# Low parts moved to other engines and places in three stages, and half of the first mapped weights split, in a decoder block on one core

## The chip, the cores and the metric

The kernel runs on one core of a Trainium2 chip. The metric is the device time of one execution in microseconds (us), as the median of several runs. The engines are TensorE (PE, matmuls and transposes; PEld is its weight load), VectorE (DVE), ScalarE (ACT), GpSimd (POOL) and SyncE (SP, which issues most of the DMAs).

## The reference

One decoder block in f32 on a sequence of 1024 tokens of width 1024, with 16 heads of 64:

```python
mod = jax.nn.silu(c) @ w_ada + b_ada
shift, scale, gate = jnp.split(mod, 3, axis=-1)
h = rms_norm(x, norm_gain) * (1.0 + scale[:, None, :]) + shift[:, None, :]
q, k, v, z_a, u, z_b, m_a, m_b = jnp.split(h @ w_in, offs, axis=-1)
attn = stick_breaking_attention(to_heads(q), to_heads(k), to_heads(v))
p_a = (attn * jax.nn.silu(z_a)) @ w_branch_a
pooled = multiscale_causal_pool(u, pool_w, pool_scale)
p_b = (pooled * jax.nn.silu(z_b)) @ w_branch_b
merged = jax.nn.sigmoid(m_a) * p_a + jax.nn.sigmoid(m_b) * p_b
return x + gate[:, None, :] * (merged @ w_out)
```

Behind the block stands a last RMS norm with its own gain. The pooling takes trailing means over 2, 4, 8 and 16 tokens, minus the token itself, then one 256x256 map for each of four groups of channels (`pool_w`).

## The kernel before

**Precision.** Nearly every matmul is made of three products. An f32 operand is split into a high part (a cast to fp32r, most often on ACT) and a low part (the f32 value less the high part, a subtraction on DVE or POOL), and PE computes high x high, high x low and low x high into one PSUM bank. So a block of weights can be used in part as soon as it is cast, and in full when its low part is there. In the names, `w_3_raw` is a block as loaded, `w_3` holds its two parts, and a row such as `wa<-wa_raw,wa` on DVE makes the low part. All matmuls are issued in one helper, at L99, so rows are told apart by their tiles.

**The front.** Four blocks of x (`x_0` to `x_3`, 128 tokens each) are loaded, squared and summed on ACT (`junk<-x`), raised to -0.5 by POOL (L245, `st`), scaled on DVE (`x<-x,st`), turned by PE in sets of four transposes (`xt`), and made into `hf` and the high part of `hT` by ACT, with the low part of `hT` by DVE. `mods` are the columns of the modulation, which DVE sums up in two operations per block of channels (`mj`), and for which ACT computes a sigmoid (`sigb`). Meanwhile PE folds the maps of the pooling into the weights of `u`: for each group g of 256 channels, `mapped(g, q, tag)` for q = 0 to 3 makes 256 columns (`wm_q`), two halves of weights (`wt_0` for q = 0, 1 and `wt_1` for q = 2, 3) against the map `praw`. ACT and DVE split each result into `wg`. Groups 0 and 1 are computed in whole f32 (`WHOLE = 2`), groups 2 and 3 in three fp32r products. The first accumulation over the eight blocks of channels, `ua`, starts when the first `hT` and `wg` are there. The front is written out by hand: `order(...)` keeps the instructions of each engine in the order of the program as long as `pinned[0]` is set. PSUM has four tags of two banks: `pj`, `z`, `av`, `tr`; `ua0` to `ua3` take `pj`, `pj`, `z`, `z`.

**Middle stages.** The projections of u and v follow, then the pooled branch (`pb`), in which the low parts of later weights are made ahead by `make_lo` and put into memory (`wl_d`). Attention runs over eight pairs of heads; its logits `z` go through two sigmoids on ACT (`om`, `be`), a select on POOL (L802), a scan on DVE (L804, `om<-om`) and a multiplication on DVE. The projections of the pairs run beside it; `load_parts(i)` loads weight tile i, and tiles below `PLAIN` are split there, low part on POOL (L114, `w<-w_raw,w`).

**The last stage.** For each half of the tokens (`sh` 0 and 1) and each j from 0 to 7, `load_w` loads and splits `wa_j`, three loads bring `s_j`, `m_j` and `b_j`, PE computes `pa_j` from `ga` and `wa_j` (24 matmuls, of which the third is the first to need `wa_j`'s low part), and DVE forms `m_j`·`b_j` + `pa_j`·`s_j` and splits it into `mhl_j`. Then the output product `o` runs from `mhl` and `wo`, with a last norm for each block of 128 tokens: `y`, squares on ACT (`t`), sums (`qq`), a power on POOL (L1014) and two multiplications on DVE (L1019). In the first half `wo` is scaled by the gate (`wor`) and split as well. The order of these instructions on each engine isn't written by hand: a scheduler sets it from its own estimate of times, and so do the buffers of the pools: a tile with `bufs=2` can't be loaded until the last reader of the tile two before is done.

Of the kernel before, what the change touches and what calls it, by code (L numbers as in the profile page):

```python
# [9 lines left out]
F32 = mybir.dt.float32  # L10
# [5 lines left out]
P = 128  # L16
# [19 lines left out]

PLAIN = 8
LO_V = (1, 0, 1, 1, 0, 1, 1, 0)
LO_ZB = (0, 1, 0, 1, 0, 1, 0, 1)
# [6 lines left out]

WHOLE, G2 = 2, 1
BUSY = 10
# [7 lines left out]
def block_kernel(ctx, tc, a, out):  # L56
    nc = tc.nc
# [5 lines left out]
    const = ctx.enter_context(pool("const"))  # L63
    big = ctx.enter_context(pool("big"))
    wts = ctx.enter_context(pool("wts"))
    dram = ctx.enter_context(tc.tile_pool(name="dram", bufs=1, space=bass.MemoryType.DRAM))
# [13 lines left out]

    ident = const.tile([P, P], F32, name="ident")
    make_identity(nc, ident)
    ones = const.tile([P, P], F32, name="ones")
    gp.memset(ones, 1.0)
# [52 lines left out]

    def make_lo(pl, n, tag=None, bufs=3):

        for _ in range(n):  # L140
            i = next(early_lo)
            if tag:
                raw, hi = (pl.tile([P, D], t_, tag=tag, bufs=5, name=f"l{i}_{n_}") for n_, t_ in (("raw", F32), ("hi", F32R)))
            else:
                raw = pl.tile([P, D], F32, tag="lraw", bufs=bufs, name=f"l{i}_raw")
                hi = pl.tile([P, D], F32R, tag="lhi", bufs=1, name=f"l{i}_hi")
            nc.sync.dma_start(raw, a["w_in"][tiles[i]])
            act.copy(hi, raw)
            v.tensor_sub(raw.bitcast(F32R), raw, hi.bitcast(F32))
            nc.sync.dma_start(wl_d[i], raw)  # L150
# [51 lines left out]
    with pool("init") as init:  # L202

        affb = const.tile([P, 8], F32, name="affb")
        v.scalar_tensor_tensor(affb, bada_v[:, 8:16], 1.0, gain_v, ALU.add, ALU.mult)

        crow = init.tile([P, D], F32, tag="vjunk", bufs=1, name="crow")[0:1]
        nc.sync.dma_start(crow, a["c_row"])
# [32 lines left out]
        def square_x(sb):  # L241
# [37 lines left out]
        xts = {}  # L279

        def turn_x(sh, kb):
            pt = xts[sh, kb] = bank(("tr", "av")[kb % 2], f"xt{sh}_{kb}")
            for i in range(4):
                transpose(pt[:, i * P:(i + 1) * P], xs[4 * sh + i][:, kb * P:(kb + 1) * P])
# [18 lines left out]

        wg, maps, halves = {}, {}, {}

# [9 lines left out]

        def split_map(g):
            hl = init.tile([P, 2, 2, 256], F32R, tag="phl", bufs=1, name=f"phl{g}")
            order(act.copy)(hl[:, 0], maps[g])
            order(v.tensor_sub)(hl[:, 1], maps[g], hl[:, 0].bitcast(F32))
            maps[g] = hl  # L320

# [5 lines left out]

        def mapped(g, q, tag):
# [4 lines left out]
            th, ml = halves[g, q // 2], maps[g]  # L333
            for e in range(2):
                ks = slice((2 * q + e) % 4 * P, (2 * q + e) % 4 * P + P)

                pairs = [(th[:, cb, ks], ml[:, cb]) for cb in range(2)] if g < WHOLE else [
                    (th[:, i, cb, ks], ml[:, j, cb]) for i, j in ((0, 0), (0, 1), (1, 0)) for cb in range(2)]
                for n, (l, r) in enumerate(pairs):
                    mm(ps[:, e * 256:e * 256 + 256], l, r, start=n == 0, stop=n == len(pairs) - 1)  # L340

            def out(which=(0, 1)):
                dst = wg[g][:, :, 2 * q:2 * q + 2].rearrange("p i k d -> p i (k d)")
                if 0 in which:
                    order(act.copy)(dst[:, 0], ps)
                if 1 in which:
                    order(v.tensor_sub)(dst[:, 1], ps, dst[:, 0].bitcast(F32))
            return out

# [60 lines left out]
        load_mod(4)  # L410
        low_h(0, 0, v)
        m13(lo_)
        make_h(0, 1, None)
# [3 lines left out]
        sl = slice(0, 512)  # L417

        def cast(g, hf):
            raw = halves[g, hf]  # L420
            hl = halves[g, hf] = wts.tile([P, 2, 2, 512], F32R, tag="whl", bufs=2, name=f"wt{g}_{hf}")
            order(act.copy)(hl[:, 0], raw)
            return lambda: order(v.tensor_sub)(hl[:, 1], raw, hl[:, 0].bitcast(F32))

        def cast_map(g):
            raws[g] = maps[g]
            maps[g] = init.tile([P, 2, 2, 256], F32R, tag="phl", bufs=1, name=f"phl{g}")
            order(act.copy)(maps[g][:, 0], raws[g])

        def low_map(g):  # L430
            order(v.tensor_sub)(maps[g][:, 1], raws.pop(g), maps[g][:, 0].bitcast(F32))

        raws = {}

# [10 lines left out]
        for kb in range(KB):  # L445
# [56 lines left out]
            if kb == KB - 2:  # L502

                turned = [init.tile([P, 4, 512], F32, tag="wa", bufs=3, name=f"xt{i}") for i in range(2)]
                for i in range(2):
                    load(turned[i].rearrange("p k s -> p (k s)"), a["x_t"][i])
                split_map(3)
                for hf in range(2):
                    split_half(3, hf)
# [33 lines left out]

    def make_d(j):
        win = WINDOWS[j // 2]
        u = dif.tile([P, S + 16], F32, tag="u", bufs=2, name=f"u{j}")
        v.memset(u[:, S:], 0.0)
        nc.sync.dma_start(u[:, :S], u_d[j])
        cur, n, step = u, S + 16, 1
# [12 lines left out]


    with pool("vp") as vp:
# [11 lines left out]
        early.close()  # L576
        diffs = ExitStack()
        dif = diffs.enter_context(pool("dif", side="right"))
        for hf in range(2):
            if hf == 0:  # L580
                wv.append([load_wv(1, k2) for k2 in range(4)])
            for sb in range(8):
# [15 lines left out]
                )  # L598
                make_lo(vp, LO_V[sb])
                if 8 * hf + sb in DIFFS:  # L600
                    make_d(DIFFS[8 * hf + sb])


    with pool("pb") as pb:
        gb = pb.tile([P, 2, KB, S], F32R, name="gb")
        for j in range(KB):
            if j not in dhls:
                make_d(j)
            zs = [pb.tile([P, 512], F32, tag="zs", bufs=3, name=f"zs{j}_{sh}") for sh in range(2)]
# [333 lines left out]
    with pool("fin") as fin:  # L943
# [138 lines left out]
```

## Time and profile before

| | us |
|---|---|
| median of 3 runs | 1212.78 (1212.56 to 1213.09) |
| the profiled execution | 1212.4 |
| its span in the trace | 1210.4 |
| PE busy | 1199.6 (99%) |
| DVE busy | 757.9 (63%) |
| ACT busy | 540.6 (45%) |
| POOL busy | 193.8 (16%) |

The granted TensorE clock was 0.999 of full speed. A row of the time line gives start and duration in us, the engine, the line, the operation, what it writes and reads, the sizes and how many instructions are merged (x16); in brackets stands the time that the engine was idle just before, and what ended that. A list of waits gives for each pair of waiter and releaser the sum in us, the number of times and the longest.

### The profile page before, as it was taken

What the parts mean: (1) busy time and instruction counts of PE and PEld (TensorE: products, weight loads), DVE (VectorE), ACT (ScalarE), POOL (GpSimd) and SP (SyncE); (2) the same over time, 40 slices, a digit from 0 to 9 for tenths busy, and PEclk for the clock granted to TensorE, in tenths of its full rate; (3) what the DMA queues carried; (4) which work ended last, traced back from release to release, by engine and by line L of the source; (5) the groups of instructions that cost most, each with busy time, mean ns of one, the idle gap of its engine ahead of it and who ended that gap; (6) DMA issues with size and microseconds to landing.
All of it is one profiled execution on the core that took longest, in us unless ns stands there. A gap on an engine that the chain in (4) does not pass through costs nothing.

```text
span 1210.4 us, 16174 instructions
## 1 busy us (share of the span) xinstructions
PE 1199.6 (99%) x5746; PEld 1000.1 (83%) x5746; DVE 757.9 (63%) x1049; ACT 540.6 (45%) x1008; POOL 193.8 (16%) x361
## 2 busy tenths in 40 slices
PE   8999999999999999999999999999999999999997
PEld 7888888888888888888888888888888888888886
DVE  6764482677410277767768677776777763785643
ACT  5564341334211265665556655655655653232211
POOL 1000000001222343212212122231211310000001
PEclk9999999999999999999999999999999999999999
DMA  9649994626846632442635325353343236984622
GB/s 361 255 168 339 326 383 167 214 82 230 317 148 117 179 92 75 133 121 78 170 109 157 113 80 153 109 158 115 106 132 102 96 126 211 315 275 168 218 65 84
DMA packets 81955, 207.13 MB, mean 171 GB/s; under 512 B 10450, under 2 KB 23890, under 8 KB 79699
## 3 DMA queue, kind: packets, MB, share of 16 engines
q1 hardware_dynamic: 73666, 191.23, 49.2%
q10 hardware_dynamic: 8208, 14.88, 3.3%
q8 instruction: 45, 0.74, 0.2%
q14 instruction: 36, 0.29, 0.1%
HBM read 138.96 MB, written 50.34 MB: 156 GB/s over the span
## 4 chain that ended last, share of the span: by engine, by line
PE 93%; DVE 2%; DMA 2%; issue 1%; ACT 0%; POOL 0%; SPq 0%; POOLq 0%; DVEq 0%; ACTq 0%
PE p L99 36%; PE pb L99 7%; PE wzb L99 7%; PE v L99 7%; PE o L99 6%; PE av L99 6%; PE z L99 6%; PE wt L99 5%; PE pa L99 5%; PE u L99 5%; PE ua L99 3%; PE wm L99 1%; DMA m<-sb_d 1%; DMA out_y<-y 0%; DMA praw<-in_pool_w 0%
## 5 line engine op out<-in xcount | busy, mean ns | idle before, releaser
L99 PE MATMUL p<-hT,w 128*128 128x512 f32 x1920 | 480.9, 392 | 0.0
L99 PEld LDWEIGHTS p<-hT,w 128*128 128x128 f32 x1920 | 354.8, 188 | 68.6
L804 DVE TENSOR_TENSOR_SCAN om<-om 128x512 f32<-128x512 f32 (+7 forms) x128 | 175.4, 1370 | 50.0 <-ACT om L797 41.5
L824 DVE TENSOR_TENSOR wt<-wt,wt 128x512 fp32r<-128x512 f32 (+1 forms) x160 | 100.5, 628 | 93.7 <-ACT wt L823 93.1
L823 ACT CAST wt<-wt 128x512 fp32r<-128x512 f32 (+1 forms) x160 | 87.5, 547 | 130.2 <-PE wt L99 129.7
L797 ACT ACTIVATE om<-z 128x512 f32<-128x512 f32 (+2 forms) x192 | 94.9, 494 | 77.2 <-PE z L99 52.2
L802 POOL TENSOR_SCALAR_AFFINE_SELECT om<-om 128x128 f32<-128x128 f32 x128 | 50.9, 397 | 364.3 <-ACT om L797 344.0
L99 PE MATMUL av<-wt,vv 128*128 128x512 f32 x320 | 106.0, 412 | 0.0
L99 DVE TENSOR_TENSOR be<-be,om 128x511 f32<-128x511 f32 (+7 forms) x128 | 95.8, 758 | 0.3
L798 ACT ACTIVATE be<-z 128x512 f32<-128x512 f32 (+2 forms) x192 | 94.2, 491 | 0.0
L99 PE MATMUL pa<-ga,wa 128*128 128x512 f32 x384 | 89.9, 390 | 0.3 <-DVE s L976 0.2
L99 PEld LDWEIGHTS wt<-ident,be 128*128 128x128 f32 x576 | 72.7, 140 | 20.9
L99 PE MATMUL o<-wo,mhl 128*128 128x512 f32 (+1 forms) x408 | 89.6, 377 | 0.0
L99 PE MATMUL wt<-ident,be 128*128 128x128 f32 x576 | 88.7, 272 | 0.0
L99 PE MATMUL v<-wv,hT 128*128 128x512 f32 x384 | 87.2, 389 | 0.0
L99 PE MATMUL wzb<-hT,wzb 128*128 128x512 f32 x384 | 87.2, 389 | 0.0
L99 PE MATMUL pb<-gb,wb 128*128 128x512 f32 x384 | 87.2, 389 | 0.0
L99 PEld LDWEIGHTS o<-wo,mhl 128*128 128x128 f32 x408 | 73.5, 188 | 14.1
L99 PEld LDWEIGHTS pa<-ga,wa 128*128 128x128 f32 x384 | 71.9, 188 | 15.9 <-issue 0.6
L99 PEld LDWEIGHTS v<-wv,hT 128*128 128x128 f32 x384 | 72.1, 188 | 14.9
L99 PEld LDWEIGHTS wzb<-hT,wzb 128*128 128x128 f32 x384 | 72.1, 188 | 14.9
L99 PEld LDWEIGHTS pb<-gb,wb 128*128 128x128 f32 x384 | 72.1, 188 | 14.9
(129 smaller groups left out, 1374.2 us busy)
## 6 DMA issues: line engine op xcount, KB each, us to landing
w_raw<-in_w_in SPq DMA_DIRECT2D x40, 512.0 KB, 4.8
l_raw<-in_w_in SPq DMA_DIRECT2D x32, 512.0 KB, 5.1
wl_d<-l_raw SPq DMA_DIRECT2D x32, 512.0 KB, 5.8
w<-wl_d SPq DMA_DIRECT2D x32, 512.0 KB, 3.9
v_d<-vo SPq DMA_DIRECT2D x16, 512.0 KB, 4.8
vv<-v_d SPq DMA_DIRECT2D x8, 1024.0 KB, 5.5
wa_raw<-in_w_branch_a SPq DMA_DIRECT2D x16, 512.0 KB, 4.8
wa<-in_w_mod SPq DMA_DIRECT2D x7, 1024.0 KB, 6.5
```

The source lines that it names most:

```text
L99: ins = op(*args, **kw)
L797: act.activation(om[:, b0:b0 + n], zp[:, :n], AF.Sigmoid, scale=-0.125)
L798: act.activation(be[:, b0:b0 + n], zp[:, :n], AF.Sigmoid, scale=0.125)
L802: gp.affine_select(out=tl[:, :P], in_=tl[:, :P], pattern=[[1, P]], compare_op=ALU.is_gt, fill=fill, base=0, channel_multiplier=-1)
L804: v.tensor_tensor_scan(om[:, :W], om[:, :W], om[:, :W], 1.0, ALU.mult, ALU.min)
L823: act.copy(wt[:, 0, :off], pt[:, :off])
L824: v.tensor_sub(wt[:, 1, :off], pt[:, :off], wt[:, 0, :off].bitcast(F32))
```

## The change

Six edits, in four places.

**Front.** A sigmoid of a small constant tile stands ahead of everything on ACT, so that its table is loaded at the start. The map of group 0 and its second half of weights are split into fp32r parts (`WHOLE` is now a list of the halves that stay whole); the first scaling of x goes from DVE to ACT; the last two mapped blocks of group 1 take the banks `av` and `tr` of the first two transposes instead of two of `z`; the second half of the last block is computed behind the first transposes, and the split of `wm_2` is moved in part behind `hT`'s first low part.

**v stage.** `make_lo` can give back its cast and subtraction to be issued one block later, and the loads of `make_d` are issued one block sooner.

**Attention.** The low part of weight tile 4 is made by DVE instead of POOL.

**Last stage.** `s_`, `m_` and `b_` have three buffers each.

```diff
+MASKED = 4
-WHOLE, G2 = 2, 1
+WHOLE = ((0, 0), (1, 0), (1, 1))
...
     def load_parts(i, name):
         if i < PLAIN:
-            return load_w(a["w_in"][tiles[i]], name, act, gp)
+            return load_w(a["w_in"][tiles[i]], name, act, v if i == MASKED else gp)
...
+        act.activation(mhalf, mhalf, AF.Sigmoid)
+        gp.memset(mhalf, -0.5)
...
+        def scale_act(sb):
+            order(act.mul)(xs[sb], xs[sb], stats[sb][:, 2:3])
...
-        mapped(0, 0, "pj")()
+        m00 = mapped(0, 0, "pj")
+        cast_map(0)
+        low_map(0)
+        m00()
+        t0_lo = cast(0, 1)
         m01 = mapped(0, 1, "pj")
+        t0_lo()
         m01(hi)
         square_x(0)
         m01(lo_)
         spread()
-        scale_x(0)
+        scale_act(0)
...
-        m12 = mapped(1, 2, "z")
-        m13 = mapped(1, 3, "z")
+        for kb in range(2):
+            bank_x(0, kb)
+        m12 = mapped(1, 2, "av")
+        m13 = mapped(1, 3, "tr", (0,))
         square_x(3)
+        m12(hi)
         scale_x(3, some)
         turn_x(0, 0)
         scale_x(3, rest)
         turn_x(0, 1)
-        m12()
         make_h(0, 0, None)
+        m13.products((1,))
         m13(hi)
         modulation(1)
         load_mod(4)
         low_h(0, 0, v)
+        m12(lo_)
         m13(lo_)
...
-                make_lo(vp, LO_V[sb])
+
+                now, todo = todo, make_lo(vp, LO_V[sb], later=True)
                 if 8 * hf + sb in DIFFS:
-                    make_d(DIFFS[8 * hf + sb])
+                    j = DIFFS[8 * hf + sb]
+                    todo.append(lambda j=j, u=load_u(j): make_d(j, u))
+                for f in now:
+                    f()
...
-                s_ = fin.tile([P, 512], F32, tag="s_", bufs=2, name=f"s{sh}_{j}")
+                s_ = fin.tile([P, 512], F32, tag="s_", bufs=3, name=f"s{sh}_{j}")
...
-                m_ = fin.tile([P, 512], F32, tag="m_", bufs=2, name=f"m{sh}_{j}")
+                m_ = fin.tile([P, 512], F32, tag="m_", bufs=3, name=f"m{sh}_{j}")
...
-                b_ = fin.tile([P, 512], F32, tag="b_", bufs=2, name=f"b{sh}_{j}")
+                b_ = fin.tile([P, 512], F32, tag="b_", bufs=3, name=f"b{sh}_{j}")
```

The following rows show the order of instructions. On PE in front, at the end of group 1's mapped blocks, before:

```order
L99 MATMUL wm_2_227<-praw_128,wt_130 128x256 x4
L99 MATMUL wm_3_232<-praw_128,wt_130 128x256 x4
L99 MATMUL xt_0_242<-ident,x_113 128x128
...
L99 MATMUL xt_1_248<-ident,x_116 128x128
L99 MATMUL ua_273<-hT,wg_143 128x512 x2
L99 MATMUL ua_274<-hT,wg_143 128x512 x2
```

and after:

```order
L103 MATMUL wm_2_256<-praw_133,wt_135 128x256 x4
L103 MATMUL wm_3_261<-praw_133,wt_135 128x256 x2
L103 MATMUL xt_0_254<-ident,x_118 128x128
...
L103 MATMUL xt_1_255<-ident,x_121 128x128
L103 MATMUL wm_3_261<-praw_133,wt_135 128x256 x2
L103 MATMUL ua_300<-hT,wg_148 128x512 x2
L103 MATMUL ua_301<-hT,wg_148 128x512 x2
```

Half of `wm_3` stands behind the two sets of transposes now, ahead of the first `ua`.

On DVE in the first half of the last stage, around the low part of `wa_3`, before:

```order
L977 TENSOR_TENSOR m_1_9509<-m_1_9509,s_1_9507 128x512
L123 CAST mhl_1_9541<-m_1_9509 128x512
L114 TENSOR_TENSOR wa_3_9588<-wa_3_raw,wa_3_9588 128x1024
L114 TENSOR_TENSOR mhl_1_9541<-m_1_9509,mhl_1_9541 128x512
L948 TENSOR_TENSOR wor_9628<-wor_9628,bg 128x1024
L948 TENSOR_TENSOR wor_9675<-wor_9675,bg 128x1024
L950 TENSOR_TENSOR wo<-wor_9628,wo 128x1024
L114 TENSOR_TENSOR wa_4_9635<-wa_4_raw,wa_4_9635 128x1024
L950 TENSOR_TENSOR wo<-wor_9675,wo 128x1024
L976 TENSOR_TENSOR s_2_9549<-pa_2_9556,s_2_9549 128x512
```

and after:

```order
L1018 TENSOR_TENSOR m_1_9536<-m_1_9536,s_1_9534 128x512
L1010 TENSOR_TENSOR m_2_9578<-m_2_9578,b_2_9580 128x512
L127 CAST mhl_1_9568<-m_1_9536 128x512
L118 TENSOR_TENSOR mhl_1_9568<-m_1_9536,mhl_1_9568 128x512
L1017 TENSOR_TENSOR s_2_9576<-pa_2_9583,s_2_9576 128x512
L118 TENSOR_TENSOR wa_3_9615<-wa_3_raw,wa_3_9615 128x1024
L989 TENSOR_TENSOR wor_9655<-wor_9655,bg 128x1024
```

`s_2<-pa_2` stood seven operations behind the low part of `wa_3`; it stands directly ahead of it now.

On DVE at the start of the second half, around the low part of `wa_2`, before (`y` is the last of the first half's four output blocks):

```order
L1003 TENSOR_TENSOR y_10074<-o_1_10106,y_10074 128x512
L976 TENSOR_TENSOR s_0_10145<-pa_0_10152,s_0_10145 128x512
L977 TENSOR_TENSOR m_0_10147<-m_0_10147,s_0_10145 128x512
L114 TENSOR_TENSOR wa_2_10226<-wa_2_raw,wa_2_10226 128x1024
L1011 SCALAR_TENSOR_TENSOR qq_10076<-qq_10076 128x1
...
L1019 SCALAR_TENSOR_TENSOR y_10074<-y_10074,qq_10076,fg 128x512 x2
```

and after:

```order
L1044 TENSOR_TENSOR y_10101<-o_1_10133,y_10101 128x512
L1017 TENSOR_TENSOR s_0_10172<-pa_0_10179,s_0_10172 128x512
L1052 SCALAR_TENSOR_TENSOR qq_10103<-qq_10103 128x1
L1018 TENSOR_TENSOR m_0_10174<-m_0_10174,s_0_10172 128x512
L1060 SCALAR_TENSOR_TENSOR y_10101<-y_10101,qq_10103,fg 128x512 x2
L118 TENSOR_TENSOR wa_2_10253<-wa_2_raw,wa_2_10253 128x1024
```

`qq` and the two `y` multiplications, which wait for POOL's power, stood behind the low part of `wa_2`; they stand ahead of it now. The edit of the v stage moves no instruction on any engine.

## Rows read from the trace of the kernel before

**Rows 1.** The page, part 1: busy us, share of the span, instructions.
```profile
PE 1199.6 (99%) x5746; PEld 1000.1 (83%) x5746; DVE 757.9 (63%) x1049; ACT 540.6 (45%) x1008; POOL 193.8 (16%) x361
```

**Rows 2.** The list of waits of PE: us in total, times, longest.
```profile
PE ua L99 <- ACT hT L99: 1.1, 1, 1.1
PE ua L99 <- DVE wg L99: 1.0, 1, 1.0
PE z L99 <- ACT be L798: 0.4, 1, 0.4
PE pa L99 <- DVE s L976: 0.2, 1, 0.2
```

**Rows 3.** The time line of PE in front.
```profile
15.12 7.07 PE L99 MATMUL wm<-praw,wt 128*128 128x256 f32 x32
...
22.03 1.04 PE L99 MATMUL xt<-ident,x 128*128 128x128 f32 x8
24.15 1.66 PE L99 MATMUL ua<-hT,wg 128*128 128x512 f32 x6 [1.08 <-ACT hT L99]
...
30.93 3.01 PE L99 MATMUL ua<-hT,wg 128*128 128x512 f32 x12
...
39.74 1.59 PE L99 MATMUL wm<-phl,wt 128*128 128x256 f32 x12
```

**Rows 4.** Tile x from 0 to 24 us: its loads, issue ns and first and last issue.
```profile
L234 SPq DMA_DIRECT2D x<-in_x x4: 328/431/463, 3.0 to 8.7; - x4
...
DMA to landing us min/median/max: 5.7/8.5/10.0
```

**Rows 5.** The time line of DVE in front.
```profile
13.34 1.29 DVE L99 TENSOR_TENSOR scb<-crow,sigb 128x512 f32<-128x512 f32 x2 [2.26 <-ACT sigb L99]
14.54 0.74 DVE L99 TENSOR_SCALAR x<-x,st 128x1024 f32<-128x1024 f32 x1
...
19.68 1.21 DVE L99 SCALAR_TENSOR_TENSOR mj<-wa,scb 128x1024 f32<-128x1024 f32 x1
...
21.67 0.88 DVE L99 TENSOR_SCALAR x<-x,st 128x128 f32<-128x128 f32 x2
...
29.08 0.69 DVE L99 TENSOR_TENSOR hT<-hf,hT 128x512 fp32r<-128x512 f32 x1
```

**Rows 6.** The time line of ACT in front.
```profile
19.26 1.06 ACT L99 ACTIVATE junk<-x 128x1025 f32<-128x1025 f32 x1
...
22.67 0.78 ACT L99 ACTIVATE hf<-xt,mods 128x512 f32<-128x512 f32 x1 [1.58 <-PE xt L99]
...
30.43 0.62 ACT L99 CAST hT<-hf 128x512 fp32r<-128x512 f32 x1
```

**Rows 7.** The time line of POOL: the power in front and in the last stage.
```profile
20.49 0.81 POOL L245 TENSOR_TENSOR st<-st,mhalf 128x1 f32<-128x1 f32 x1 [2.56 <-ACT junk L99]
...
1127.46 0.66 POOL L1014 TENSOR_TENSOR qq<-qq,mhalf 128x1 f32<-128x1 f32 x1 [6.88 <-DVE qq L1011]
```

**Rows 8.** The time lines of POOL and DVE early in attention.
```profile
426.85 2.40 POOL L114 TENSOR_TENSOR w<-w_raw,w 128x1024 fp32r<-128x1024 f32 x1 [0.20 <-ACT w L119]
...
429.53 1.02 DVE L804 TENSOR_TENSOR_SCAN om<-om 128x384 f32<-128x384 f32 x1 [2.39 <-POOL om L802]
```

**Rows 9.** The time line of PE in the last stage, from 1039 us on.
```profile
1038.74 11.95 PE L99 MATMUL pa<-ga,wa 128*128 128x512 f32 x52
```

**Rows 10.** The time line of DVE in the last stage, first half.
```profile
1039.84 0.69 DVE L976 TENSOR_TENSOR s<-pa,s 128x512 f32<-128x512 f32 x1 [1.20 <-PE pa L99]
...
1043.05 1.22 DVE L114 TENSOR_TENSOR wa<-wa_raw,wa 128x1024 fp32r<-128x1024 f32 x1
```

**Rows 11.** The time line of DVE in the last stage, start of the second half.
```profile
1124.16 0.69 DVE L1003 TENSOR_TENSOR y<-o,y 128x512 f32<-128x512 f32 x1 [4.75 <-PE o L99]
...
1126.10 1.22 DVE L114 TENSOR_TENSOR wa<-wa_raw,wa 128x1024 fp32r<-128x1024 f32 x1
...
1129.97 1.41 DVE L1019 SCALAR_TENSOR_TENSOR y<-y,qq,fg 128x512 f32<-128x512 f32 x2
```

More of the change, by code (lines that the diff above doesn't have):

```diff
@@ L64, in block_kernel @@
     big = ctx.enter_context(pool("big"))
+    idp = ctx.enter_context(pool("idp"))
     wts = ctx.enter_context(pool("wts"))
@@ L79, in block_kernel @@
     wl_d = dram.tile([5 * KB, P, D], F32, name="wl_d")
-    ident = const.tile([P, P], F32, name="ident")
+    ident = idp.tile([P, P], F32, name="ident")
     make_identity(nc, ident)
-    ones = const.tile([P, P], F32, name="ones")
+    ones = idp.tile([P, P], F32, name="ones")
     gp.memset(ones, 1.0)
@@ L136, in block_kernel, with make_lo @@
     early_lo = iter(range(PLAIN, len(tiles)))
-    def make_lo(pl, n, tag=None, bufs=3):
+    def make_lo(pl, n, tag=None, bufs=3, later=False):
+        rest = []
         for _ in range(n):
@@ L147, in make_lo, with low @@
             nc.sync.dma_start(raw, a["w_in"][tiles[i]])
-            act.copy(hi, raw)
-            v.tensor_sub(raw.bitcast(F32R), raw, hi.bitcast(F32))
-            nc.sync.dma_start(wl_d[i], raw)
+            def low(i=i, raw=raw, hi=hi):
+                act.copy(hi, raw)
+                v.tensor_sub(raw.bitcast(F32R), raw, hi.bitcast(F32))
+                nc.sync.dma_start(wl_d[i], raw)
+            if later:
+                rest.append(low)
+            else:
+                low()
+        return rest
     def load_parts(i, name):
         if i < PLAIN:
-            return load_w(a["w_in"][tiles[i]], name, act, gp)
+            return load_w(a["w_in"][tiles[i]], name, act, v if i == MASKED else gp)
         raw = wts.tile([P, KB, P], F32, tag="raw", bufs=2, name=name + "_raw")
@@ L279, in block_kernel, with bank_x @@
         xts = {}
+        def bank_x(sh, kb):
+            xts[sh, kb] = bank(("tr", "av")[kb % 2], f"xt{sh}_{kb}")
         def turn_x(sh, kb):
-            pt = xts[sh, kb] = bank(("tr", "av")[kb % 2], f"xt{sh}_{kb}")
+            if (sh, kb) not in xts:
+                bank_x(sh, kb)
+            pt = xts[sh, kb]
             for i in range(4):
@@ L302, in block_kernel @@
         tags = ("pj", "pj", "z", "z", "av", "tr")
-        wg, maps, halves = {}, {}, {}
+        wg, maps, parts_m, halves = {}, {}, {}, {}
         def load_map(g):
@@ L314, in load_half, with cast_map, low_map, cast @@
             halves[g, hf] = raw.rearrange("p (c k) -> p c k", c=2)
[L316 to L320, printed above, removed]
+        def cast_map(g):
+            parts_m[g] = init.tile([P, 2, 2, 256], F32R, tag="phl", bufs=1, name=f"phl{g}")
+            order(act.copy)(parts_m[g][:, 0], maps[g])
+        def low_map(g):
+            order(v.tensor_sub)(parts_m[g][:, 1], maps[g], parts_m[g][:, 0].bitcast(F32))
+        def cast(g, hf):
+            raw = halves[g, hf]
+            hl = halves[g, hf] = wts.tile([P, 2, 2, 512], F32R, tag="whl", bufs=2, name=f"wt{g}_{hf}")
+            order(act.copy)(hl[:, 0], raw)
+            return lambda: order(v.tensor_sub)(hl[:, 1], raw, hl[:, 0].bitcast(F32))
         def split_half(g, hf):
@@ L326, in split_half, with mapped @@
             order(v.tensor_sub)(hl[:, 1], raw, hl[:, 0].bitcast(F32))
-        def mapped(g, q, tag):
+        def mapped(g, q, tag, es=(0, 1)):
             if g not in wg:
@@ L332, in mapped, with products @@
             ps = bank(tag, f"wm{g}_{q}")
[L333 to L340, printed above, removed]
+            th = halves[g, q // 2]
+            whole = (g, q // 2) in WHOLE
+            ml = maps[g] if whole else parts_m[g]
+            def products(es):
+                for e in es:
+                    ks = slice((2 * q + e) % 4 * P, (2 * q + e) % 4 * P + P)
+                    pairs = [(th[:, cb, ks], ml[:, cb]) for cb in range(2)] if whole else [
+                        (th[:, i, cb, ks], ml[:, j, cb]) for i, j in ((0, 0), (0, 1), (1, 0)) for cb in range(2)]
+                    for n, (l, r) in enumerate(pairs):
+                        mm(ps[:, e * 256:e * 256 + 256], l, r, start=n == 0, stop=n == len(pairs) - 1)
+            products(es)
             def out(which=(0, 1)):
@@ L347, in out @@
                     order(v.tensor_sub)(dst[:, 1], ps, dst[:, 0].bitcast(F32))
+            out.products = products
             return out
@@ L417, in block_kernel @@
         sl = slice(0, 512)
[L419 to L433, printed above, removed]
         def hi_products(todo):
@@ L506, in block_kernel @@
                     load(turned[i].rearrange("p k s -> p (k s)"), a["x_t"][i])
-                split_map(3)
+                cast_map(3)
+                low_map(3)
                 for hf in range(2):
@@ L542, in block_kernel, with load_u @@
     dhls = {}
-    def make_d(j):
-        win = WINDOWS[j // 2]
+    def load_u(j):
         u = dif.tile([P, S + 16], F32, tag="u", bufs=2, name=f"u{j}")
@@ L548, in make_d @@
         nc.sync.dma_start(u[:, :S], u_d[j])
+        return u
+    def make_d(j, u):
+        win = WINDOWS[j // 2]
         cur, n, step = u, S + 16, 1
@@ L577, in block_kernel @@
         diffs = ExitStack()
+        todo = []
         dif = diffs.enter_context(pool("dif", side="right"))
@@ L598, in block_kernel @@
                 )
-                make_lo(vp, LO_V[sb])
+                now, todo = todo, make_lo(vp, LO_V[sb], later=True)
                 if 8 * hf + sb in DIFFS:
-                    make_d(DIFFS[8 * hf + sb])
+                    j = DIFFS[8 * hf + sb]
+                    todo.append(lambda j=j, u=load_u(j): make_d(j, u))
+                for f in now:
+                    f()
+        assert not todo
     with pool("pb") as pb:
```

2 lines of the change are left out of this document (1 added, 1 removed).

## The prediction

> **What bounds the kernel now.** I read the page's busy shares first, then the list of who TensorE (PE) waits for, then the stretches of the time line around each of those waits. PE is busy 1199.6 us of the 1210.4 us span [rows 1]: a change can only bring what is left of PE's idle time, or shorten PE's own work. The list of its waits [rows 2] has few entries that an order of instructions can move: 1.1 us at the first products of `ua` (for `hT`, from ACT), 1.0 us a little later (for a `wg` part, from DVE), 0.4 us in attention (for `be`) and 0.2 us in the last stage (for `s`). Between them PE runs without a gap, so what is gained or lost at one place reaches the end in full, unless DVE or a load gives it back at once. The pace of PE in the last stage is (11.95 - 0.39)/51 = 0.227 us per 128x512 matmul [rows 9]; one takes 0.39 from start to end.
>
> **The front (0 to 45 us).** PE's own work: `wm_2` and `wm_3` of group 0 go from 16 f32 records to 24 in fp32r. 32 f32 records took 7.07 us and 12 fp32r ones 1.59 [rows 3], so 3.5 becomes 3.0, -0.5. The same row gives 0.22 per f32 record, and four of them (`wm_3`'s second half) leave the stretch ahead of the transposes, another -0.9 there; they are done while PE waits for `hT`, which is the cover. PE would thus reach the first transposes at about 20.6 instead of 22.03 [rows 3]. It can't use all of that. The fourth x block is issued at 8.7 and lands 10.0 later [rows 4], at 18.7; its Square and the read behind it end 1.25 later (1.06 and some 0.2, [rows 6]), its power takes POOL 0.81 [rows 7]; that is 20.8, and DVE is then just through `wg` and scales the first 128 columns by 21.2 (before: from 21.67, [rows 5]). The transpose ends at 21.5, the ACT step `hf` starts there instead of at 22.67 [rows 6], and the first `ua` product, which stood 1.48 behind it [rows 3, 6], comes at 23.0 instead of 24.15: -1.15. The next wait, 1.00 for DVE's `wg` [rows 2], was for the bank of the last map block; that block now has another bank, so this wait goes and a gain of 2.15 would stand at 27 us.
>
> What is late next is DVE's chain of `mj`, `hT` and `wg` operations, which has no gap from 21.67 on. DVE loses one scaling (0.74) to ACT; the two operations it gains (the low parts of the map and of the weights, by their sizes 0.69 and 1.22, [rows 10]) fall into its idle time ahead of `scb`, of which the last piece alone was 2.26 us [rows 5], so they cost nothing. One `wg` part, some 0.69 by its size, is moved behind the first `hT` low part. With the 0.5 by which the last scaling comes sooner, that first `hT` part comes 1.2 earlier, but from the next one on, with the `wg` part made up for, DVE is only some 0.55 ahead of before. The second `hT` low part, which ended at 29.77 [rows 5], then ends at 29.2, while PE is there at 23.0 + 24 products and two sets of transposes (5.4 + 0.7) at 28.5 to 29.1 with its own wait for the second high part: a stall of 0.3 to 0.7. The third high part, whose cast ended at 31.05 [rows 6], ends at 30.5, and PE wants it at 30.1. Its first products after that come at 30.5, where before they came four matmuls behind 30.93 [rows 3], at 31.84. I keep -1.3 for the front. The bounds are -0.55 (PE tied to DVE all the way) and -2.15. The second table load of ACT and the moved scaling are off the path: ACT waits 1.58 for PE ahead of `hf` [rows 6].
>
> **The v stage.** The helper that holds back the low parts by one block gives the same sequence on every engine between the front and attention. Zero.
>
> **Attention.** `w_4`'s low part moves from POOL, where it took 2.40 us [rows 8], to DVE, where such a subtraction takes 1.22 [rows 10]. The two selects queued behind it on POOL let DVE's scan start at 429.53, after 2.39 us of idle time that now hold the subtraction [rows 8]. The scan starts about 1.1 us earlier, which is more than the 0.4 that PE waits behind it. -0.4, between 0 and -0.5.
>
> **The last stage.** Three buffers instead of two for `s_`, `m_` and `b_` let the third set of loads go out ahead of the weights `wa_3`. The wait of 0.2 behind `m`·`b` on the way to `s` goes [rows 2]. But the scheduler also moves DVE's operations, and two of the new places stand badly, since DVE takes its queue in order.
>
> First half: `s_2`, which waits for the end of `pa_2`, now stands directly ahead of `wa_3`'s low part. Before, that part ran at 1043.05 [rows 10]. PE's stretch of 52 matmuls begins with the last four of `pa_1` [rows 9], so `pa_2`'s last one ends at 1038.74 + 27 x 0.227 + 0.39 = 1045.25, and `pa_3`'s third product, the first that needs the low part, stands at 1038.74 + 30 x 0.227 = 1045.54. Now DVE starts `s_2` at 1045.3, is through at 1045.95 (0.69, [rows 10]) and through `wa_3`'s low part 1.22 later, at 1047.15 to 1047.2. PE stands 1.65 us. Nothing covers it, since PE's order has nothing between. +1.65, at most +1.8 with a restart, and 0 at the least if the row of work ahead were to change.
>
> Second half: `qq`, `m_0` and both `y` operations of the fourth output block now stand ahead of `wa_2`'s low part (before: behind). The last product of that output block ends at 1124.13 (`y` starts at 1124.16, [rows 11]). Fifteen matmuls now stand ahead of the one that needs the low part: 1123.97 + 3.4 = 1127.37. DVE: Square and read on ACT, the small POOL operation and `qq` end at about 1126.1, the power on POOL takes 0.66 [rows 7] to 1126.75, the two `y` 1.41 [rows 11] to 1128.2, the low part to 1129.35. A stall of 2.0. Before, the low part ended at 1127.32 [rows 11] against 14 matmuls, 1127.14, a loss of 0.2. Net +1.75, bounds 0.9 (if `y` ran without the power's wait) and 2.2.
>
> How long the power takes there depends on what DVE does meanwhile. In the front the power at 20.49 lasted 0.81 and ended 0.41 behind the `mj` operation, which had run from 19.68 to 20.89 [rows 5, 7]. The Trainium skill (SBUF — State Buffer, "Who interferes with whom") says why that may be: a DVE instruction with two inputs in SBUF and a GpSimd one that reads SBUF shut each other out for a whole instruction, whichever was first. By that rule `m_0`, which has two such inputs, would hold the power back until 1126.7 and the stall would be 2.4 and the sum 0.4 higher; the trace agrees in the front, no row shows this pair.
>
> **The sum.** -1.3 - 0.4 - 0.2 + 1.65 + 1.75 = +1.5. The profiled execution took 1212.4, its span is 1210.4; so 1213.9 with a span of 1211.9. The median of the runs is 1212.78, 0.4 above the profiled one, and by it the forecast is 1214.2 us.
>
> **The rivals.** (a) The new stalls of the last stage are covered, as the moved operations come out earlier than I have them or PE arrives later. For it speaks that the loads come sooner, against it that both stalls are counted from the end of a PE product, in operations whose durations have rows. Only the gains stay: 1212.78 - 1.3 - 0.4 - 0.2 = 1210.9, and 1210.0 with the front's full 2.15. (b) The change doesn't do in front what it says: DVE's chain, which has no gap, swallows the gain of PE there. It decides at a front gain under about 0.35, from which the time is over 1215.2; at none it is 1215.5, slower than before. For it speaks that DVE comes out only 0.55 ahead and has the low parts of the next group's map and weights still to make, on which PE could wait again; against it that the 1.00 was for a bank, not for the chain. (c) The stalls are longer: the power held back (0.4), or one more low part late at the end of the first half, where I find 1 to 4 us of room. 1215.0 to 1216.2. (d) The wait in attention stays, +0.4 on any case.
>
> **How the numbers follow.** Forecast 0.50, from 1212.6 to 1215.2; (a) 0.18; (b) 0.17; (c) 0.15. Within 0.2% means 2.4 us to either side, 1210.4 to 1215.2, about what a measurement of this kernel can tell from no change. Faster by more needs (a) with the larger front gain: 0.12. Slower by more is most of (b), the upper part of (c) and the edge of the forecast: 0.27. The rest, 0.61, is no change. The range leaves out the far end of (a) and of (c): 1210.5 to 1216.0.
>
> **What would show it.** In front: first `ua` product at 23.0, no wait for `wg` behind it but short ones for `hT`, the third k block's products at 30.5. In attention: the scan of the block at 428.4 less the front's gain, no PE wait for `be`. In the last stage: two new waits of PE for `wa`'s low part from DVE, 1.65 and 2.0 us, one in each half, and none for `s`. It would be wrong if those two are missing, if the front gives over 2 or under 0.5, or if PE shows a new wait at any third place.

## The result

The changed kernel took 1217.13 us (median of 6 runs, 1215.64 to 1219.88) against 1213.07 us before, a ratio of 1.0036 with a 95% interval of 1.0025 to 1.0047. It is slower by 4.1 us where the forecast had 1.4: 2.9 above the forecast's 1214.2 and beyond the upper end of its range, 1216.0. A second measurement, beside other runs of before, gave 1217.64 against 1212.70, 1.0038 (1.0024 to 1.0052).

The profiled execution took 1217.4 us with a span of 1215.3. The starts of some products of PE in three traces, one of the kernel before and two of the changed one, say in which stage the time went:

| start, us | before | changed | changed, second trace |
|---|---|---|---|
| first `v` | 128.15 | 128.28 | 127.60 |
| first `p` (attention) | 389.26 | 389.40 | 388.72 |
| first `pa` (last stage) | 1028.76 | 1028.67 | 1027.99 |
| last product | 1203.86 | 1208.84 | 1208.16 |

So the front and the projections brought +0.13 in one trace and -0.55 in the other, attention -0.23 in both (639.50 to 639.27), and the last stage lost 5.07 in both (175.10 to 180.17).

The list of waits of PE in the changed kernel, beside [rows 2]:

```profile
PE pa L103 <- DVE wa L118: 3.7, 2, 2.2
...
PE ua L103 <- ACT hf L103: 0.2, 1, 0.2
PE ua L103 <- ACT hT L103: 0.2, 1, 0.2
PE ua L103 <- DVE hT L103: 0.2, 1, 0.2
```

Of the four waits of [rows 2], that for `hT` from ACT is down to 0.2 us, with two others of 0.2 beside it, and the other three are gone, as the change meant; in their place stand two for `wa`'s low part. The time line of PE shows both, in the answer to [rows 9], and below it in the second half:

```profile
1039.77 5.83 PE L103 MATMUL pa<-ga,wa 128*128 128x512 f32 x25
1047.06 5.28 PE L103 MATMUL pa<-ga,wa 128*128 128x512 f32 x22 [1.46 <-DVE wa L118]
...
1125.39 3.56 PE L103 MATMUL pa<-ga,wa 128*128 128x512 f32 x15
1131.19 7.13 PE L103 MATMUL pa<-ga,wa 128*128 128x512 f32 x23 [2.23 <-DVE wa L118]
```

From start to start, the first costs 1047.06 - (1039.77 + 5.83 - 0.39) - 0.23 = 1.62 us, and the second, by the same sum, 2.40. The last row has a third loss in it: 23 products at the pace of 0.227 take 5.4 us, and these took 7.13; 0.1 of that is the first product behind the wait, which takes longer. The busy time in steps of a microsecond tells why (its last three columns are the granted clock, as a share of 2.4 GHz, the DMA share and GB/s):

```profile
1131.00:1132.00 1.00, 0.81 (x4) 0.69 (x5) 1.00 (x4) 0.00 (x0) 0.00 (x0) 1.00 0.75 281
1132.00:1133.00 1.00, 1.00 (x5) 0.81 (x4) 1.00 (x2) 0.00 (x0) 0.00 (x0) 0.80 0.80 98
1133.00:1134.00 1.00, 1.00 (x3) 0.72 (x3) 1.00 (x3) 0.00 (x0) 0.00 (x0) 0.50 0.90 356
...
1135.00:1136.00 1.00, 1.00 (x4) 0.81 (x3) 0.59 (x1) 0.00 (x0) 0.00 (x0) 0.50 0.96 340
1136.00:1137.00 1.00, 1.00 (x5) 0.80 (x5) 0.00 (x0) 0.00 (x0) 0.00 (x0) 0.99 1.04 356
```

PE stood for 2.2 us, worked for 1.4 us at 2.4 GHz, and then ran at 1.2 GHz from 1132.6 to 1136.0 us. In that time eight products were stretched by 0.2 each, 1.6 us in all.

DVE's time lines, beside [rows 10] and [rows 11], show the operations in the places that the order gave them:

```profile
1045.18 0.69 DVE L1017 TENSOR_TENSOR s<-pa,s 128x512 f32<-128x512 f32 x1 [0.94 <-PE pa L103]
1045.79 1.22 DVE L118 TENSOR_TENSOR wa<-wa_raw,wa 128x1024 fp32r<-128x1024 f32 x1
...
1127.33 0.15 DVE L1052 SCALAR_TENSOR_TENSOR qq<-qq 128x1 f32<-128x1 f32 x1
1127.45 0.69 DVE L1018 TENSOR_TENSOR m<-m,s 128x512 f32<-128x512 f32 x1
1128.59 1.41 DVE L1060 SCALAR_TENSOR_TENSOR y<-y,qq,fg 128x512 f32<-128x512 f32 x2 [0.44 <-POOL qq L1055]
1129.92 1.22 DVE L118 TENSOR_TENSOR wa<-wa_raw,wa 128x1024 fp32r<-128x1024 f32 x1
```

In front, beside [rows 3], [rows 5] and [rows 6] (PE, then DVE, then ACT):

```profile
11.63 4.36 PE L103 MATMUL wm<-phl,wt 128*128 128x256 f32 x24
15.78 6.54 PE L103 MATMUL wm<-praw,wt 128*128 128x256 f32 x28
22.15 1.17 PE L103 MATMUL xt<-ident,x 128*128 128x128 f32 x8
...
24.27 2.12 PE L103 MATMUL ua<-hT,wg 128*128 128x512 f32 x8
...
22.06 0.88 DVE L103 TENSOR_SCALAR x<-x,st 128x128 f32<-128x128 f32 x2
...
29.48 0.68 DVE L103 TENSOR_TENSOR hT<-hf,hT 128x512 fp32r<-128x512 f32 x1
...
20.25 1.06 ACT L103 ACTIVATE junk<-x 128x1025 f32<-128x1025 f32 x1
...
30.94 0.62 ACT L103 CAST hT<-hf 128x512 fp32r<-128x512 f32 x1
```

The 24 fp32r products took 4.36 us instead of 3.0, because here too the clock was low, from 13.0 to 16.4 us:

```profile
12.00:13.00 1.00, 1.00 (x11) 1.00 (x10) 1.00 (x2) 1.00 (x2) 0.17 (x1) 1.00 0.92 320
13.00:14.00 1.00, 1.00 (x7) 1.00 (x6) 0.27 (x1) 1.00 (x3) 0.00 (x0) 0.52 0.96 365
...
15.00:16.00 1.00, 1.00 (x6) 1.00 (x6) 0.96 (x3) 0.09 (x2) 0.83 (x1) 0.50 1.03 422
16.00:17.00 1.00, 1.00 (x5) 0.83 (x5) 0.76 (x2) 0.98 (x2) 0.31 (x1) 0.78 1.03 422
```

In the changed kernel the fourth block of x is scaled at 22.06, where it was scaled at 21.67 before, instead of the forecast's 21.2, and the first `ua` product comes at 24.27 instead of the forecast's 23.0 (24.15 before).

### The profile page after: what moved, and what is told of

The parts are those of the page before. It is cut to its first block, busy times and chain, and to the rows that moved or that the text cites. A ratio compares the mean times of both kernels' runs of the same rounds, so it can differ in the third digit from the quotient of the medians.

```text
span 1215.3 us, 16180 instructions
## 1 busy us (share of the span) xinstructions
PE 1203.2 (99%) x5754; PEld 1002.7 (82%) x5754; DVE 761.9 (63%) x1051; ACT 543.3 (45%) x1011; POOL 192.6 (16%) x361
## 4 chain that ended last, share of the span: by engine, by line
PE 96%; DVE 1%; issue 1%; DMA 1%; ACT 0%; POOL 0%; POOLq 0%; DVEq 0%; ACTq 0%
PE p L103 36%; PE wzb L103 7%; PE v L103 7%; PE pb L103 7%; PE pa L103 7%; PE o L103 6%; PE z L103 6%; PE av L103 6%; PE wt L103 5%; PE u L103 5%; PE ua L103 2%; PE wm L103 2%; DMA wa<-in_w_mod 1%; DVE mj L103 1%; PE idle L103 0%
```

## The experiments

Four questions were open: what each part is worth alone; whether the last stage's loss is all DVE's order; whether the low clock or DVE's chain took the front's gain; and whether the clock's fall belongs to the order of instructions.

### Each part alone

**The front alone**: the change with POOL making `w_4`'s low part and two buffers in the last stage.

```diff
-MASKED = 4
+MASKED = -1
...
-                s_ = fin.tile([P, 512], F32, tag="s_", bufs=3, name=f"s{sh}_{j}")
+                s_ = fin.tile([P, 512], F32, tag="s_", bufs=2, name=f"s{sh}_{j}")
```

> The edits of the front and the v stage alone, on the kernel before. Theory clock: PE's granted clock falls to the lower level between 13 and 17 us as in the changed kernel, ACT's third Square is pushed back to 20.2 us, and the front gives -0.2 to +0.2 us (1213.1 us). If the clock does not fall in an execution, that execution shows the first ua product near 23.0 and gives -1.3 (1211.8). Rival chain (b of the prediction): ua comes at 23.0 to 23.5 with the clock at full speed and the gain is lost later in waits for hT; also 1213 us, but with no row below full clock.

Measured: 1212.40 against 1212.70, ratio 0.9997 (0.9989 to 1.0006). The clock was low here as well in the traced execution, from 12.6 to 16.1 us. The front is worth nothing that can be measured. Each execution's mean granted clock is known too: the traced one, with its fall, has 0.997, and the eight at 0.999 or 1.000 have a median of 1212.2 us. So even without the fall the front gives some 0.5 by the medians, not the 1.3 that was expected of such executions.

**The last stage alone**: the kernel before, with `bufs=3` for `s_`, `m_` and `b_`.

> Only the third buffers of s_, m_ and b_, on the kernel before. Theory: two waits of PE for wa's low part, 1.6 us near 1045 and 2.4 near 1128, less the 0.7 of waits of before that go, +3.3; and if the clock falls to the lower level behind the second one, as in the changed kernel, 1.5 more: 1216.4 to 1217.9 us. Rival (the stalls are a matter of the shifted front): under +1.

Measured: 1218.11, ratio 1.0044 (1.0031 to 1.0056). The whole loss is here. In its trace the two waits are 1.6 and 2.4 us and the last stage 3.5 us longer than before. The clock did not fall behind the second wait this time; instead PE had two waits of 0.7 from start to start in the `v` stage, which the trace of before has not; from the first `v` to the first `p` that stage is 1.8 us longer (262.88 against 261.12). The list of waits of PE:

```profile
PE pa L99 <- DVE wa L114: 3.7, 2, 2.2
...
PE v L99 <- DVE vo L594: 1.1, 2, 0.6
```

The time line of DVE at the first of them:

```profile
154.45 1.24 DVE L553 TENSOR_TENSOR win<-u 128x1039 f32<-128x1039 f32 x1 [1.39 <-DMA u<-u_d]
155.60 0.68 DVE L594 TENSOR_TENSOR vo<-v,vo 128x512 fp32r<-128x512 f32 x1
```

DVE stood at `win<-u` for a load, and `vo`, for which PE waits, stood behind it. No instruction of that stage differs from the kernel before, so this comes and goes with the arrival of the load: it was issued at 147.3 and landed at 154.4 here, at 146.7 and 151.7 in the trace of before.

**All but the last stage**: the change with two buffers.

> The changed kernel with two buffers again in the last stage (front, v stage and attention stay). Theory clock: -0.5 for attention and the front's 0 with the clock low at 13 to 17 us: 1212.5 us; with the clock at full speed 1211.2. Rival (all of the loss is in the front): 1215 us or more.

Measured: 1211.40, ratio 0.9988 (0.9979 to 0.9997), 1.0 below the front alone. In the traces attention took 639.26 here, 639.50 before and 639.95 in the front alone, whose wait for `be` of 0.4 is there as before. So `w_4`'s low part on DVE is worth 0.2 to 0.7 by the trace that one compares with, and the rest of that 1.0 is within what medians of these kernels scatter.

### The last stage: order or buffers

**Low products last**: everything of the change stays, DVE's order at `s_2` and `wa_3` too, but PE takes the products that need the low part at the end of each `pa_j`.

```diff
-                for p in range(NP):
-                    for w, m in ((whl[0], ga[p][:, 0]), (whl[0], ga[p][:, 1]), (whl[1], ga[p][:, 0])):
-                        mm(ps, w[:, p], m, start=n == 0, stop=n == 23)
-                        n += 1
+                todo = [(whl[0], p, i) for p in range(NP) for i in range(2)] + [(whl[1], p, 0) for p in range(NP)]
+                for w, p, i in todo:
+                    mm(ps, w[:, p], ga[p][:, i], start=n == 0, stop=n == 23)
+                    n += 1
```

> The changed kernel, but in each pa_j the eight products that need wa_j's low part stand last, so PE has 16 matmuls (3.6 us) of work ahead of the first of them instead of 2 (0.45). Theory DVE order: both waits for wa's low part (1.6 and 2.4 us) go, and with them the clock's fall behind the second: -5 against the changed kernel, 1211.5 to 1212.3 us, as with two buffers, or 0.4 better for the waits near 1157. Rival (the third buffers cost elsewhere, for instance by their loads): 1214 us or more with no wait for wa.

Measured: 1210.94, ratio 0.9985 (0.9977 to 0.9994); 6.2 below the changed kernel. PE's row of the last stage is whole again, without a wait:

```profile
1039.76 12.40 PE L103 MATMUL pa<-ga,wa 128*128 128x512 f32 x54
```

The last stage took 174.27 us from the first `pa` to the last product, 5.9 less than in the changed kernel and 0.8 less than before. The rival, a cost of the third buffers as such, falls. In the first half DVE's operations around `wa_3` stand in the changed kernel's order (`s` at 1044.95, the low part at 1045.55), so there PE's order alone took the wait away. In the second half the scheduler has moved more: no product of `o` stands between the first blocks of `pa` any more, and `y` stands ahead of `s` and `m`. The end of the second wait is therefore not shown to be the work of PE's order of products alone.

**The same with two buffers.**

> The same order of products, with two buffers of s_, m_ and b_ (front, v stage and attention of the change stay). Theory: the waits of 0.34 near 1127 and 0.45 near 1157 of before go at most: 1210.6 to 1211.4 us. Compared with the kernel with three buffers and this order it prices the third buffers alone: 0 to 0.4 in favour of three by the theory, over 1 in favour of two by the rival.

Measured: 1211.27, ratio 0.9986 (0.9978 to 0.9995), the last stage 174.28 us. The third buffers by themselves are worth nothing once PE's order has room; the same few lines bring two buffers to the same length.

**One half mended at a time** (`if sh == 0:` or `if sh == 1:` around the new order, the old order in the other half).

> The changed kernel with wa's low products last in the first half of the tokens only: of the two new waits only the second stays. Theory: 2.4 us near 1128 and, in the executions in which the clock falls behind it, 1.5 more: 1213.4 to 1215 us, 2.5 to 4 above the kernel in which both halves are mended (1210.9). Rival (the loss is the sum of many small ones): about half of 6.

> The same in the second half only: the first wait stays. Theory: 1.7 us near 1045 and no fall of the clock behind it: 1212.6 us, 1.7 above the kernel in which both halves are mended.

Measured: with the first half mended 1213.18, 2.2 above both halves mended; with the second half mended 1212.27, 1.3 above. Neither trace has a low clock in the last stage. Together this makes 3.5 of the 6.2. The second wait is shorter here, 1.6 us in the list, because the scheduler now puts `y` ahead of `m_0`, so that POOL's power isn't held up (it took 0.55, from 1124.83 on, beside `s`, where it took 0.98 beside `m_0`):

```profile
1124.58 0.16 DVE L1055 SCALAR_TENSOR_TENSOR qq<-qq 128x1 f32<-128x1 f32 x1 [0.93 <-ACT t L1051]
1124.78 0.69 DVE L1020 TENSOR_TENSOR s<-pa,s 128x512 f32<-128x512 f32 x1
1125.41 1.41 DVE L1063 SCALAR_TENSOR_TENSOR y<-y,qq,fg 128x512 f32<-128x512 f32 x2
1126.74 0.68 DVE L1021 TENSOR_TENSOR m<-m,s 128x512 f32<-128x512 f32 x1
1127.35 1.22 DVE L118 TENSOR_TENSOR wa<-wa_raw,wa 128x1024 fp32r<-128x1024 f32 x1
```

The rest of the 6.2 is, by the traces, the longer second wait (2.4 against 1.8 from start to start) and the low clock behind it (1.6), neither of which the traces with one half mended have; 0.5 is within the scatter of the medians.

### The front: clock or chain

**crow moved ahead of the second mapped block**, so that f32 products stand between these one-row products and the fp32r ones.

```diff
+        spread_pe()
         m01 = mapped(0, 1, "pj")
         t0_lo()
         m01(hi)
         square_x(0)
         m01(lo_)
         spread()
```

> The changed kernel with PE's two small products of c (crow, one row of the array) moved ahead of the second mapped block, so that whole f32 products stand between them and the fp32r ones. Theory clock, cause crow then fp32r: the clock stays at full speed at 13 to 17 us, ua starts near 23.0 and the time falls by 1.2 to 1.5 against the changed kernel: 1215.7 us. Rival (the fp32r products alone let the clock fall): no difference, 1217.1. Rival chain: ua near 23.0 but the time unchanged.

Measured: 1218.06, ratio 1.0045 (1.0033 to 1.0058), so the expected gain did not come. The clock was at 2.4 GHz throughout the front, and yet the first `ua` came at 25.0. PE reached the transposes at 20.63 and stood there:

```profile
14.54 6.26 PE L103 MATMUL wm<-praw,wt 128*128 128x256 f32 x28
20.63 0.69 PE L103 MATMUL xt<-ident,x 128*128 128x128 f32 x3
23.19 0.92 PE L103 MATMUL xt<-ident,x 128*128 128x128 f32 x5 [1.86 <-DVE x L103]
```

The moved products delayed `wm_1` and with it the queues of ACT and DVE.

**crow ahead of all mapped blocks**, with two buffers in the last stage (`spread()` moved ahead of `m00`).

> Two buffers in the last stage, the split kept, and crow with its sigmoids ahead of the first mapped block. f32 products stand between crow and the fp32r ones. Theory clock: full speed at 10 to 17 us; DVE's scb is done 5 us earlier, Square of the fourth x block is at its landing (18.9 to 19.3), ua starts at 23.0 to 23.5: -1.0 to -1.5 against the kernel with crow in its place, 1210.0 us. Rival chain: ua at 23.5 but the waits for hT grow by as much: 1211.4.

Measured: 1212.94 (1212.01 to 1217.30), ratio 1.0008 (1.0000 to 1.0017), 1.5 worse than with `crow` in its place and 2.9 above what was expected, although in the trace the clock was at full speed: the fourth block of x was scaled at 22.85 and `u` started at 70.50.

**The second half of group 0 whole again**, two buffers.

```diff
-WHOLE = ((0, 0), (1, 0), (1, 1))
+WHOLE = ((0, 0), (0, 1), (1, 0), (1, 1))
...
-        cast_map(0)
-        low_map(0)
         m00()
-        t0_lo = cast(0, 1)
         m01 = mapped(0, 1, "pj")
-        t0_lo()
```

> Two buffers in the last stage, and the second half of group 0's weights kept whole, as f32 products (16 records instead of 24, no map split, no weight split in front); the rest of the front's edits stay. Theory clock: without fp32r products behind crow the clock stays at full speed at 12 to 17 us as before the change, Square of the fourth x block is at 18.9 to 19.3 where it lands, ua starts at 23.2 to 23.8 and the front gains 0.5 to 1.2 against the kernel with the split: 1210.5 us. Rival chain: PE's own 0.5 is lost and nothing else changes: 1211.4 to 1212.

Measured: 1211.55, ratio 0.9991 (0.9983 to 1.0000). Clock at full speed, scaling at 21.02, `u` 0.83 earlier than before, and yet the median is that of the kernel with the split (1211.40), as the rival had it.

**The fourth x block loaded earlier**, with both halves mended and group 0 whole.

```diff
         load_x(2)
+        load_x(3)
         load_mod(0, [slice(1, 2)])
         load_half(1, 1, t1[:, 1])
-        load_x(3)
```

> Both halves mended, three buffers, group 0's second half whole, and the fourth x block loaded ahead of the second half of the first modulation block and of group 1's last weights, so that it lands 2.5 us earlier, at 16.2 to 17. Theory DVE chain in front (what follows starts a fixed time behind the scaling of the fourth x block): the scaling starts at 20.3 to 21.0 instead of 21.6, u starts 0.6 to 1.3 earlier than in the kernel before, 1210.2 us. Rival (the loads that are pushed back, 512 KB each, take its place): u where it is, 1211.

Measured: 1211.65, ratio 0.9988 (0.9980 to 0.9997). The scaling started at 20.95 and `u` at 68.68, both as expected; the Square itself ran at 19.13, since ACT had it behind the cast of a mapped block. The time was not lower than with both halves mended alone (1210.94), and 1.4 above what was expected; the trace shows one wait of 1.6 us in the `v` stage, of the kind seen above, with DVE 2.39 us idle for the load of `u`.

**The changed kernel once more.**

> The changed kernel once more, unchanged, for a second trace. Theory: the two waits for wa's low part are there again with 1.6 and 2.4 us; u starts 47.8 +- 0.2 us behind the fourth x block's scaling; whether the clock falls in front and behind the second wait differs from execution to execution. Rival (the fall belongs to the order of instructions): both falls at the same places as before. 1216 to 1218 us.

Measured: 1217.64. The two waits of the last stage have the same length, and the clock is low behind the second one again:

```profile
1131.00:1132.00 1.00, 1.00 (x6) 0.77 (x5) 1.00 (x2) 0.00 (x0) 0.00 (x0) 0.78 0.42 74
1132.00:1133.00 1.00, 1.00 (x4) 0.81 (x3) 1.00 (x2) 0.00 (x0) 0.00 (x0) 0.50 0.88 311
...
1135.00:1136.00 1.00, 1.00 (x6) 0.84 (x5) 0.00 (x0) 0.00 (x0) 0.00 (x0) 1.00 0.56 221
```

In front it is at full speed this time, with the same instructions, and the first `ua` is at 23.5.

All the traces together answer the front. From the scaling of the fourth x block to the first `u`:

| kernel | scaling, us | first `u`, us | between |
|---|---|---|---|
| x3 loaded earlier | 20.95 | 68.68 | 47.73 |
| half whole, two buffers | 21.02 | 68.75 | 47.73 |
| second half mended | 21.09 | 68.75 | 47.66 |
| changed, second trace | 21.35 | 69.11 | 47.76 |
| first half mended | 21.51 | 69.26 | 47.75 |
| low products last | 21.58 | 69.50 | 47.92 |
| last stage alone (the front of before) | 21.65 | 69.57 | 47.92 |
| before | 21.67 | 69.58 | 47.91 |
| low products last, two buffers | 21.85 | 69.60 | 47.75 |
| changed | 22.06 | 69.75 | 47.69 |
| front alone | 22.06 | 69.85 | 47.79 |
| all but the last stage | 22.50 | 70.16 | 47.66 |
| crow first of all | 22.85 | 70.50 | 47.65 |
| crow ahead of second block | 22.86 | 70.51 | 47.65 |

The distance is 47.65 to 47.92 whether the clock fell or not and whatever PE did in between. So the end of the front is set by what starts with this scaling, and the rows make that DVE's chain: it has no gap for 18 us from there on. No run took an operation out of the chain, so this is read from the rows and the distances. The clock counts by moving the scaling: of the eight traces with the changed kernel's front, the three with the fall (changed, front alone, all but the last stage) have it at 22.06 to 22.50, the other five at 21.09 to 21.85, though the fourth x block landed no sooner in these (19.1 to 20.0 against 19.1 to 19.6).

## Why the prediction was wrong

**Front, -1.3: wrong, by 1.4 in the profiled execution.** Two steps of it failed. The first is the scaling at 21.2, which came at 22.06. It took the landing at 18.7 [rows 4] as fixed. In each of the thirteen traces with this order of loads the fourth x load goes out 0.02 us behind the landing of the first one, and in the trace after, the last x issue is at 9.9 instead of 8.7:

```profile
L250 SPq DMA_DIRECT2D x<-in_x x4: 328/460/611, 3.0 to 9.9; - x4
...
DMA to landing us min/median/max: 6.9/9.1/9.7
```

Here the low clock came on top: it held back `wm_1` of group 1, and the Square stood on ACT behind that block's cast, until 20.25.

The second failed step is "I keep -1.3": the account ends at the third block. From the scaling on DVE has the same operations before and after, only in another order, so that its next `mj` pair starts 5.0 behind the scaling in both traces. DVE's lead is then that of the scaling alone, as the forecast's "some 0.55 ahead" nearly had it; in the profiled execution it is a lag of 0.4 (21.67 to 22.06). What the account left out is a later place at which PE meets this chain. Before, PE came there at 44.42, 0.4 behind the end of ACT's `hf` (44.05), and did not wait. In the changed kernel it waited for `hf`, which in turn stood behind a column of `mods` that waits for DVE's `mj` (PE before, then ACT and PE after):

```profile
44.42 4.71 PE L99 MATMUL ua<-hT,wg 128*128 128x512 f32 x20
...
42.91 0.39 ACT L103 ACTIVATE mods<-acc,affb,vecs 128x1 f32<-128x1 f32 x1 [1.90 <-DVE mj L103]
...
43.67 0.78 ACT L103 ACTIVATE hf<-xt,mods 128x512 f32<-128x512 f32 x1
...
44.50 4.87 PE L103 MATMUL ua<-hT,wg 128*128 128x512 f32 x20 [0.20 <-ACT hf L103]
```

So whatever PE has won by then beyond DVE's lead and that 0.4 is lost here. With the half whole and two buffers, where the scaling is at 21.02, PE came to this place at 43.46, waited 0.2 all the same, and `u` began 0.83 sooner than before. It is rival (b), DVE's chain. With the scaling at the forecast's 21.2 and the 47.7 us from there to `u`, the front would have given 0.7, not 1.3; at the first `u`, 0.2 later than before, about 0.9 of the miss is the scaling's and 0.6 that of the later wait.

**v stage, 0.** Right: there is no difference in the order. The waits that some traces show there are those for a load; they occur with the old code of that stage (the last stage alone) as with the new (the fourth x block loaded earlier).

**Attention, -0.4: right in kind, its size between 0.2 and 0.7.** The wait for `be` is gone and the scan starts 0.94 earlier than in [rows 8], in a stage that began 0.14 later. The stage is 0.23 shorter than in the trace of before, and 0.68 shorter than in that of the front alone. The select ahead of the scan, which took POOL 0.29 at 429.21 before, now runs beside DVE's subtraction and takes 1.20:

```profile
427.19 1.22 DVE L118 TENSOR_TENSOR w<-w_raw,w 128x1024 fp32r<-128x1024 f32 x1
428.59 1.02 DVE L845 TENSOR_TENSOR_SCAN om<-om 128x384 f32<-128x384 f32 x1 [0.19 <-POOL om L843]
...
427.36 1.20 POOL L843 TENSOR_SCALAR_AFFINE_SELECT om<-om 128x128 f32<-128x128 f32 x1 [0.58 <-ACT om L838]
```

**Last stage, first half, +1.65: right.** 1.62, and 0.11 for the restart.

**Last stage, second half, net +1.75: 2.16.** The mis-sized term is POOL's power, for which the sum took 0.66 [rows 7]. It took 0.98, and ended at 1128.55, 0.41 behind the end of `m_0` on DVE:

```profile
1127.57 0.98 POOL L1055 TENSOR_TENSOR qq<-qq,mhalf 128x1 f32<-128x1 f32 x1 [5.55 <-DVE qq L1052]
```

This is what the Trainium skill (SBUF — State Buffer, "Who interferes with whom") says of a DVE instruction with two inputs in SBUF and a GpSimd one that reads SBUF: the one that comes second stands until the first is through. The trace agrees here and at the select above, and the prediction's other value for this wait, 2.4, was the measured one.

**The wait near 1157, -0.2: -0.45** from start to start. It is gone in the changed kernel.

**What no step had: the clock, +1.6.** The forecast priced a wait of PE by its length, with a restart of 0.15 at most. Behind the second wait TensorE ran at 1.2 GHz for some 3.4 us in both traces of the changed kernel. The mean granted clock of its ten executions points the same way: the two at 0.999 took 1215.64 and 1216.14 us, the eight at 0.995 to 0.998 took 1216.74 to 1219.88.

By these terms the last stage is 1.73 + 2.50 - 0.34 - 0.45 + 1.6 = 5.04 of the 5.07 measured (the two waits with 0.1 each for the restart, less what stood near 1127 and 1157 before, and the clock). Against the forecast's +1.5 for the whole, the front adds 1.4, the clock 1.6, the second wait 0.4, attention 0.2 and the first wait 0.1, less 0.25 at 1157; that is +4.95, the difference of the spans.

What stays open: in the single traces of the last stage alone and of `crow` ahead of the second block, the clock did not fall behind the same wait of 2.4 us, and both had waits elsewhere (0.7 to 0.9 each, in `v` or `pb`) that the changed kernel's traces have not. Their medians are still 5 us above that of before, and which of the two makes it up in the executions that left no trace isn't settled. One of the last stage alone, 1218.11 us at a mean granted clock of 0.999, speaks for the waits, since a fall of 3.4 us takes 0.0014 off that mean. Nor is it settled why the median of the kernel with the earlier x load isn't below that of low products last, while its front ends 0.8 earlier.

## What to carry to other kernels

When buffers are added, read the new order of the engines that take their queue in turn, not only the loads: an operation that waits for the end of a block must not stand ahead of one that the next block needs within two products. The cheap cure is on the waiting engine's side: the products that need the late part go to the end of the block, and 16 products ahead of them gave 3.6 us of room; between the two kernels that was 6 us here, of which the scheduler's other new places in the second half are a part. In a front that is full of loads and bound by a chain of one engine, find the operation that the chain starts with and measure the distance from it; PE's idle time there is no measure of what can be won.

## What was not expected of the hardware

TensorE's clock fell to 1.2 GHz in places where PE was busy, a little after a stretch in which it was not, or had only products of one row. Behind the last stage's wait of 2.4 us it fell in two of four traces; behind the other waits for `wa` of 1.6 to 1.8 us in none of six. In front, where two one-row products stood ahead of fp32r ones, it fell in three of eight traces of the same instructions, and in none of the six where whole f32 products followed the one-row ones. These counts are small and can be chance: of the twelve executions with `crow` ahead of all mapped blocks, where f32 products followed, two without a trace have a mean granted clock of 0.997 and 0.996, so it fell somewhere in them too. What is shown is that the same program can have it or not, and that a wait can cost more than its length: 1.6 us on 2.4.

The landing of one and the same load scattered: the last x block was issued between 8.6 and 10.1 us and landed between 18.6 and 20.0 in thirteen traces of kernels with the same order of loads.
